# The up-projection of a decoder layer in seeded PSUM banks, with the convolution kept in PSUM

## The chip, the cores and the metric

The kernel runs on one core of one Trainium2 chip. The metric is the device time of one execution in microseconds (us). The profile names the engines PE (TensorE), DVE (VectorE), ACT (ScalarE), POOL (GpSimd) and SP (SyncE, which here issues most transfers). PSUM, the memory into which TensorE writes, is used in eight banks of 128 partitions by 512 floats; SBUF is the memory that the other operands lie in.

## What is computed

One layer of a decoder trunk on 1024 positions of width 1024 in float32: two attention branches, gated and added to the input, then the part that matters here, a gated feed-forward block with a causal depthwise convolution of width 3:

```python
def conv_ffn(xn, w_up, conv_w, conv_b, w_down):
    S = xn.shape[1]
    u = xn @ w_up
    upad = jnp.pad(u, ((0, 0), (CONV_WIDTH - 1, 0), (0, 0)))
    c = conv_b
    for j in range(CONV_WIDTH):
        c = c + upad[:, j:j + S] * conv_w[j]
    gate, val = jnp.split(c, 2, axis=-1)
    return (jax.nn.silu(gate) * val) @ w_down
```

`xn` is the residual stream after an RMS norm, `w_up` is 1024 by 5632 (2816 columns for the gate, 2816 for the value), `w_down` 2816 by 1024. A last RMS norm follows.

## The kernel before

Everything is kept transposed: channels on the 128 partitions, the 1024 positions along the free axis. Each float32 factor is split into a high part of reduced precision (a copy by ScalarE) and a low part (the difference, by VectorE), and a product takes three matmuls per 128 rows of depth: high by high, high by low, low by high (`product`, L828). A matmul has 512 columns.

`hidden` (L839) is the up-projection. It loops over 22 pairs `j`; a pair is one block of 128 gate channels and the matching block of 128 value channels. A pair's two by two blocks (gate and value rows, first and second half of the positions) are computed by Winograd's form of Strassen's scheme, with 7 products of half depth instead of 8. Each product is 12 matmuls into one PSUM bank. In `prods` they are P1 = A11 B11, P2 = A12 B21, P5 = S1 T1, P7 = S3 T3, P3 = S4 B22, P6 = S2 T2 and P4 = A22 T4, where A are blocks of the weights, B of the activations, S sums of A and T sums of B. From pair 1 on TensorE does them in the order P1 P2 P5 P6 P7 P3 P4, the last pair ending with P4 P3.

`recombine` (L389) joins the seven banks: ScalarE copies P1 to SBUF (L395), and seven VectorE operations of 512 columns (L396 to L402) form the four blocks c11, c12 (gate, both halves) and c21, c22 (value). These land in two tiles `us` of 1024 columns, two more at the left for the convolution's past.

`glu` (L950) and `conv` (L962) then work on 1024 columns at a time. For each of the two row blocks GpSimd (VectorE for pair 0's gate) multiplies by the row scale of the norm, `rstd` (L965); ScalarE makes `c` = weight times `us` plus bias (L970); VectorE adds the two other taps (L971, L972). ScalarE applies Silu to the gate's `c` (L957), VectorE multiplies the two (L958), and a transfer on SyncE's queue stores the result to `hd` in DRAM (L959). The row scale itself is spread over the partitions during pair 0, by transposes on TensorE (L173) into two banks.

The weights come from `next_w` (L62) through `ahead`, `sum_pair` (L86) and `split_pair` (L102): two loads per pair (L91 and L93, on SyncE's queue), the four sums S by GpSimd (L96 to L99), casts by ScalarE (L110) and low parts by VectorE (L112). A11 and A12 share one tile `wh` with its low part `wl`; A22 has another; there are two buffers of these, and three for the sums `sh` and `sl`.

The order on each engine is not written out. The framework's scheduler puts the instructions into each engine's queue by priority (program order, raised by `high_priority`) and by when it expects them to be ready; `issue_after` and `add_manual_dep` add edges. On the chip each queue runs in its order and waits by semaphores. The pool `psF` gives TensorE's eight banks under one tag.

`down` (L975) follows: its first stage multiplies blocks of `hd` that are ready by weight pieces (L1023), while the last deferred `glu` calls of the up-projection run.

## Time and profile before

| | us |
|---|---|
| median of 3 runs | 1357.51 (1356.43 to 1357.77) |
| the profiled execution | 1356.2 |
| its span, first to last instruction | 1354.3 |
| pair 1's first matmul, from the span's start | 706.26 |
| the down-projection's first matmul | 1111.07 |

A row of a timeline gives start and duration in us, engine, line, operation, output and inputs, and in brackets the idle time before it with what ended that. A row of a group gives line, engine, operation, shapes and count, then the busy time in us, the mean duration in ns, and the idle time of the engine before them. A row of the waits gives who waited for whom, the total in us, how often, and the longest. A row of the windows gives a stretch, then its length and the busy time (with instructions) of PE, PEld (weight loads), DVE, ACT and POOL, the granted TensorE clock and two figures of the transfers. Where a row names `t`, it is a PSUM bank of the up-projection; B and T name the activation operands, wh, wl, sh, sl the weights.

### The profile page before, as it was taken

The page shows a single profiled execution, that of the slowest core. Times are in us where ns is not written, and L with a number is a line of the kernel's source. Part 1 is how long each engine was busy: PE and PEld are TensorE (multiplying, and loading weights), DVE is VectorE, ACT ScalarE, POOL GpSimd, SP SyncE. Part 2 cuts the span into 40 slices and gives each one's busy share as a digit, 9 for nine tenths or more (in the row PEclk, how much of TensorE's full clock was granted, in tenths as well). Part 3 has the DMA queues.
Part 4 walks back from the last instruction along what each step waited for, and adds up shares of the span by engine and source line. Part 5 has one row for each costly group of instructions (what it writes and reads, how often), then busy time and mean ns, then how long its engine had stood idle before and what let it go on. Part 6 is the DMA issues. An engine that isn't in the chain of part 4 may idle for free.

```text
span 1354.3 us, 17160 instructions
## 1 busy us (share of the span) xinstructions
PE 1335.0 (99%) x6304; PEld 1103.6 (81%) x6304; DVE 1009.8 (75%) x1454; ACT 603.9 (45%) x942; POOL 483.1 (36%) x350
## 2 busy tenths in 40 slices
PE   7999999999999999999999999999999999999997
PEld 6888888888887777878888888888888888888886
DVE  8846775388898875355689888888888898986454
ACT  8422232376667664334444334433443345433343
POOL 0436651010102125741455565555555611231011
PEclk9999999999999999999999999999999999999999
DMA  6334443966554235334422222122212248651342
GB/s 255 140 113 164 143 156 114 272 174 175 156 133 144 77 116 219 117 119 136 166 82 88 71 91 94 62 79 93 93 63 83 92 141 311 215 177 64 94 134 85
DMA packets 62470, 179.50 MB, mean 133 GB/s; under 512 B 6833, under 2 KB 15153, under 8 KB 62385
## 3 DMA queue, kind: packets, MB, share of 16 engines
q1 hardware_dynamic: 50928, 160.98, 36.7%
q10 hardware_dynamic: 11456, 17.41, 3.5%
q8 instruction: 50, 0.82, 0.2%
q14 instruction: 36, 0.29, 0.1%
HBM read 129.61 MB, written 48.76 MB: 132 GB/s over the span
## 4 chain that ended last, share of the span: by engine, by line
PE 62%; DVE 17%; POOL 7%; issue 7%; DMA 4%; ACT 3%; POOLq 0%; DVEq 0%; SPq 0%; ACTq 0%
PE t L836 7%; PE t L837 7%; PE t L835 7%; POOL us L965 3%; PE y L996 3%; PE d L996 3%; PE sc L568 3%; PE g L150 2%; PE g L151 2%; DVE c L958 2%; PE g L152 2%; DVE wl L112 2%; DMA gr<-gd 2%; PE sc L151 2%; PE sc L152 2%
## 5 line engine op out<-in xcount | busy, mean ns | idle before, releaser
L970 ACT ACTIVATE c<-us,vecs 128x1024 f32<-128x1024 f32 x44 | 54.8, 1248 | 163.2 <-POOL us L965 160.0
L965 POOL TENSOR_TENSOR us<-us,rstd 128x1024 f32<-128x1024 f32 x42 | 100.7, 2414 | 52.8 <-DVE wl L131 34.3
L110 ACT CAST sh<-sf 128x1024 fp32r<-128x1024 f32 x62 | 64.9, 1051 | 106.2 <-POOL sf L97 61.8
L129 ACT CAST wh<-raw 128x1024 fp32r<-128x1024 f32 (+2 forms) x60 | 60.7, 1012 | 104.8 <-PE sc L151 33.1
L971 DVE SCALAR_TENSOR_TENSOR c<-us,vecs,c 128x1024 f32<-128x1024 f32 x44 | 67.1, 1527 | 51.9 <-ACT c L970 51.9
L131 DVE TENSOR_TENSOR wl<-raw,wh 128x1024 fp32r<-128x1024 f32 (+2 forms) x60 | 75.3, 1256 | 39.1 <-ACT wh L129 29.3
L96 POOL TENSOR_TENSOR sf<-rv 128x512 f32<-128x512 f32 x30 | 42.5, 1417 | 166.7 <-DMA rv<-in_w_up 73.2
L112 DVE TENSOR_TENSOR sl<-sf,sh 128x1024 fp32r<-128x1024 f32 x62 | 88.3, 1426 | 8.2 <-ACT sh L110 8.2
L167 POOL TENSOR_TENSOR rs<-ms,mhalf 128x8 f32<-128x8 f32 (+2 forms) x9 | 14.5, 1614 | 159.1 <-DVE ms L165 148.5
L150 PE MATMUL g<-xh,wh 128*128 128x512 f32 x176 | 70.7, 402 | 0.1
L152 PE MATMUL g<-xh,wl 128*128 128x512 f32 x176 | 70.4, 400 | 0.0
L151 PE MATMUL g<-xl,wh 128*128 128x512 f32 x176 | 70.4, 400 | 0.0
L98 POOL TENSOR_TENSOR sf<-raw,rv 128x512 f32<-128x512 f32 x30 | 41.6, 1386 | 59.9 <-DVE sl L112 59.9
L572 DVE CUSTOM_DVE_ANT_0 L<-sc,bias 128x128 f32<-128x128 f32 (+7 forms) x64 | 47.7, 752 | 17.4 <-PE sc L568 14.1
L551 POOL MEMSET aT<- 128x128 f32 x32 | 6.1, 204 | 152.0 <-PE t L597 101.6
L573 ACT ACTIVATE L<-L,sm 128x128 f32<-128x128 f32 (+7 forms) x64 | 49.6, 778 | 20.7 <-DVE sm L572 18.2
L97 POOL TENSOR_TENSOR sf<-sf,raw 128x512 f32<-128x512 f32 x31 | 58.0, 1870 | 1.6
L972 DVE SCALAR_TENSOR_TENSOR c<-us,vecs,c 128x1024 f32<-128x1024 f32 x44 | 56.2, 1279 | 0.6
L725 POOL TENSOR_TENSOR gr<-gr,rstd 128x1024 f32<-128x1024 f32 x16 | 39.4, 2467 | 41.4 <-DMA gr<-gd 41.2
L112 DVE TENSOR_TENSOR wl<-raw,wh 128x1024 fp32r<-128x1024 f32 (+1 forms) x35 | 52.8, 1508 | 0.1
L151 PE MATMUL sc<-ml,wh 128*128 128x512 f32 x128 | 50.1, 391 | 0.6 <-DVE ml L746 0.6
L568 PE MATMUL sc<-u,u 128*128 128x512 f32 (+2 forms) x192 | 49.8, 359 | 0.1
(444 smaller groups left out, 4351.4 us busy)
## 6 DMA issues: line engine op xcount, KB each, us to landing
u<-qd SPq DMA_DIRECT2D x72, 256.0 KB, 6.1
raw<-in_w_down SPq DMA_DIRECT2D x27, 512.0 KB, 3.7
raw<-in_w_in SPq DMA_DIRECT2D x25, 512.0 KB, 4.4
hr<-hd SPq DMA_DIRECT2D x50, 256.0 KB, 5.3
raw<-in_w_up SPq DMA_DIRECT2D x23, 512.0 KB, 3.6
hd<-c SPq DMA_DIRECT2D x22, 512.0 KB, 2.8
rv<-in_w_up SPq DMA_DIRECT2D x21, 512.0 KB, 3.5
gr<-gd SPq DMA_DIRECT2D x16, 512.0 KB, 3.6
```

Source lines behind the costliest of these rows:

```text
L112: nc.vector.tensor_tensor(lo, src, hi.bitcast(F32), ALU.subtract)
L131: self.lo = (eng or nc.vector).tensor_tensor(wl, raw, wh.bitcast(F32), ALU.subtract)
L150: nc.tensor.matmul(ps, wh[:, kc + o, :], ah, start=first and n == 0, stop=False)
L151: nc.tensor.matmul(ps, wh[:, kc + o, :], al, start=False, stop=False)
L152: nc.tensor.matmul(ps, wl[:, kc + o, :], ah, start=False, stop=last and n == len(kcs) - 1)
L568: nc.tensor.matmul(sc[:, lo + n0:lo + n1], qs, k[c][part][:, n0:n1], start=part == 0, stop=part == 1)
L835: nc.tensor.matmul(ps, ah[:, k, :], bh, start=first and n == 0, stop=False, skip_group_check=skip)
L836: nc.tensor.matmul(ps, ah[:, k, :], bl, start=False, stop=False, skip_group_check=skip)
L837: nc.tensor.matmul(ps, al[:, k, :], bh, start=False, stop=last and n == len(ks) - 1, skip_group_check=skip)
L965: i = (nc.vector if m % NF == 0 else nc.gpsimd).tensor_tensor(us[:, 2:], us[:, 2:], self.rstd, ALU.mult)
L971: nc.vector.scalar_tensor_tensor(c, us[:, 1:T + 1], cw[1], c, ALU.mult, ALU.add)
L996: nc.tensor.matmul(ps, v[:, n, :], x, start=n == i == 0, stop=n == len(js) - 1 and i == 2)
```

## The change

From pair 1 on the seven products are no longer kept in seven banks and joined by VectorE, but joined as they are made, in four banks a, b, c, d. `begin` makes P1 in a; ScalarE copies a to b (the seed); TensorE makes P5 in d. `chain` adds P6 to b, which then holds P1 + P6; ScalarE copies b to c. TensorE then adds P4 of the pair before to that pair's c, and P2 to a, P7 to c, P3 to b. So its order is P1 P5 P6, P4 of the pair before, P2 P7 P3. VectorE takes the four blocks out of the banks: two are multiplied by the row scale on the way (`scaled`), two get P5 added from a copy `s5` that ScalarE made of d (`summed`) and are then multiplied by the row scale on GpSimd. T4 changes its sign, so that P4 is added; the three lines outside `hidden` do that.

The convolution of pairs 1 to 20 goes in two halves of 512 columns, with `c` in two PSUM banks (`psC`) and not in SBUF; Silu and the gate product read them there. The Silu and the second half's first step are to be issued after the seed of the next pair. The gate block's convolution is called after the next pair's first two products, the value block's after P4. Pair 0 is joined as before. The deferred calls (the value block of pair 20 and both blocks of pair 21) keep their places; those in `down` use SBUF and are no longer scaled there. The pool has seven banks under one tag and one under another, which the sum of squares, the spread of the row scale (both halves in turn) and one bank of `psC` use.

```diff
@@ -284,7 +284,7 @@
                 tt(a, a2, a, ALU.subtract)
                 tt(a2, b2, a2, ALU.subtract)
                 tt(b2, b2, a, ALU.subtract)
-                tt(b, b2, b, ALU.subtract)
+                tt(b, b, b2, ALU.subtract)
 
             def parts(k):
                 for n, r in enumerate((k, k + 4)):
@@ -399,7 +399,7 @@
         tt(c22, ps["P5"], u3, ALU.add)
         tt(u4, ps["P5"], u2, ALU.add)
         tt(c12, ps["P3"], u4, ALU.add)
-        tt(c21, u3, ps["P4"], ALU.subtract)
+        tt(c21, ps["P4"], u3, ALU.add)
 
     def keep(self, m, u, to):
 
@@ -823,7 +823,7 @@
         tt(b12, b22, b12, ALU.subtract)
         put("T13", xw[k])
         tt(t2, b22, b11, ALU.subtract)
-        tt(t4, t2, b21, ALU.subtract)
+        tt(t4, b21, t2, ALU.subtract)
 
     def product(self, ps, a, b, ks=range(4), first=True, last=True, skip=False):
 
@@ -840,15 +840,15 @@
         nc, tc = self.nc, self.tc
         with ExitStack() as ctx:
             e = ctx.enter_context
-            psF = e(tc.tile_pool(name="psF", bufs=8, space=PSUM, reuse_waits="tile"))
-            self.psT = psF
+            psF = self.psT = e(tc.tile_pool(name="psF", bufs=7, space=PSUM, reuse_waits="tile"))
+            self.psC = None
             xc2 = e(tc.tile_pool(name="xc2", bufs=1, side="right", reuse_waits="tile"))
             self.uw = e(tc.tile_pool(name="uw", bufs=3, side="right", reuse_waits="tile"))
             prods = (("P1", "A11", "B11"), ("P2", "A12", "B21"), ("P5", "S1", "T1"), ("P7", "S3", "T3"),
                      ("P3", "S4", "B22"), ("P6", "S2", "T2"), ("P4", "A22", "T4"))
             with tc.high_priority(400):
                 w0 = self.split_pair(*pair)
-            ready = {}
+            ready, prev = {}, None
             for j in range(NF):
                 w, ps = ready.pop(j) if j else (w0, {})
                 if j == 0:
@@ -861,7 +861,7 @@
                         self.B["T4", k], self.B["T2", k] = ((hi[:, c], lo[:, c]) for c in (slice(0, H2), slice(H2, T)))
                     self.tctx.close()
                     tp = e(tc.tile_pool(name="tp", bufs=2, side="right", reuse_waits="tile"))
-                    ssq = self.tl(psF, [P, H2], "t")
+                    ssq = self.tl(psF, [P, H2], "s", bufs=1)
                     for n, (name, a, b) in enumerate(prods[:5]):
                         self.product(ps[name], w[a], b, (3,), first=False)
                         if n == 4:
@@ -876,20 +876,24 @@
                                 h = self.tl(self.uw, [P, 2, H2], ("sh", "sl", "rv", "rv", "sh", "sl")[2 * k + hf], F32R, **({"bufs": 2} if k == 1 else {}))
                                 self.hs[hf, k] = self.split(h[:, 0], h[:, 1], r[:, hf * H2:(hf + 1) * H2])
                         lo = self.lo
-                for name, a, b in (prods[i] for i in ((0, 1, 2, 5, 3, 6, 4) if j == NF - 1 else (0, 1, 2, 5, 3, 4, 6) if j else range(7))):
-                    if name not in ps:
-                        ps[name] = self.tl(psF, [P, H2], "t")
-                        self.product(ps[name], w[a], b)
-                us = [self.tl(tp, [P, T + 2], "us", bufs=3) for _ in range(2)]
-                if j == NF - 1:
-                    self.defer.pop(0)(lo)
-                    self.xctx2.close()
-                    self.uw = None
-                    self.open_down()
-                    self.deep = True
-                    with tc.high_priority(100):
-                        self.ahead(2)
-                self.recombine(ps, us, tp, 2)
+                if j == 0:
+                    for name, a, b in prods:
+                        if name not in ps:
+                            ps[name] = self.tl(psF, [P, H2], "t")
+                            self.product(ps[name], w[a], b)
+                    us = [self.tl(tp, [P, T + 2], "us", bufs=3) for _ in range(2)]
+                    self.recombine(ps, us, tp, 2)
+                else:
+                    us, last = self.chain(w, ps or self.begin(psF, w), tp, prev)
+                    if j == NF - 1:
+                        self.defer.pop(0)(lo)
+                        self.xctx2.close()
+                        self.uw = None
+                        self.open_down()
+                        self.deep = True
+                        with tc.high_priority(100):
+                            self.ahead(2)
+                        last()
                 if j < NF - 1:
 
                     w, ps = ready[j + 1] = self.next_w(), {}
@@ -897,21 +901,76 @@
                         raw = [self.tl(self.sfp[0], [P, T], "t42", bufs=1)] + [self.tl(self.sfp[0], [P, T], "sf") for _ in range(2)]
                         for k, r in enumerate(raw):
                             nc.sync.dma_start(r, self.hd[k])
-                    for name, a, b in prods[:2 if j == 0 else 0]:
-                        ps[name] = self.tl(psF, [P, H2], "t")
-                        self.product(ps[name], w[a], b)
                 if j == 0:
+                    ps.update(self.begin(psF, w))
                     for hf in range(2):
-                        sp = self.tl(psF, [P, H2], "t")
+                        sp = self.tl(psF, [P, H2], "s", bufs=1)
                         self.spread(sp, rs, hf * 4)
                         nc.scalar.copy(self.rstd[:, hf * H2:(hf + 1) * H2], sp)
 
-                for w in range(2):
-                    f = lambda after=None, j=j, w=w, us=us: self.glu(j, w, us[w], tp, after)
-                    if j + w < NF - 1:
-                        f()
-                    else:
-                        self.defer.append(f)
+                first, second = (lambda after=None, j=j, w=w, us=us: self.glu(j, w, us[w], after, j > 0) for w in range(2))
+                if j == NF - 1:
+                    self.defer += [first, second]
+                elif j == 0:
+                    first()
+                    second()
+                else:
+                    prev = first, last, second
+                    if j == NF - 2:
+                        self.defer.append(second)
+                        prev = first, last, lambda: None
+            self.psC = None
+
+    def begin(self, pool, w):
+
+        ps = {n: self.tl(pool, [P, H2], "t") for n in "adbc"}
+        self.product(ps["a"], w["A11"], "B11", skip=True)
+        self.seed = self.nc.scalar.copy(ps["b"], ps["a"])
+        self.product(ps["d"], w["S1"], "T1")
+        return ps
+
+    def chain(self, w, ps, tp, prev):
+
+        nc = self.nc
+        tt = nc.vector.tensor_tensor
+        a, b, c, d = (ps[n] for n in "abcd")
+        us = [None, None]
+
+        def half(r, hf):
+            if us[r] is None:
+                us[r] = self.tl(tp, [P, T + 2], "us", bufs=3)
+            return us[r][:, 2 + hf * H2:2 + hf * H2 + H2], self.rstd[:, hf * H2:(hf + 1) * H2]
+
+        def scaled(r, hf, p):
+            u, rs = half(r, hf)
+            tt(u, p, rs, ALU.mult)
+
+        def summed(r, hf, p):
+            u, rs = half(r, hf)
+            tt(u, p, s5, ALU.add)
+            nc.gpsimd.tensor_tensor(u, u, rs, ALU.mult)
+
+        s5 = self.tl(tp, [P, H2], "s1", bufs=1)
+        nc.scalar.copy(s5, d)
+        if prev:
+            self.psC = [self.tl(self.psT, [P, H2], "s", bufs=1), self.tl(self.psT, [P, H2], "t")]
+            prev[0]()
+        self.product(b, w["S2"], "T2", first=False, skip=True)
+        nc.scalar.copy(c, b)
+        for f in prev[1:] if prev else ():
+            f()
+        self.product(a, w["A12"], "B21", first=False, skip=True)
+        scaled(0, 0, a)
+        self.product(c, w["S3"], "T3", first=False, skip=True)
+        summed(1, 1, c)
+        self.product(b, w["S4"], "B22", first=False, skip=True)
+        summed(0, 1, b)
+
+        def last():
+            self.product(c, w["A22"], "T4", first=False, skip=True)
+            scaled(1, 0, c)
+
+        return us, last
 
     def open_down(self):
         tc = self.tc
@@ -947,30 +1006,41 @@
         tt(b21, b22, b21, ALU.subtract)
         self.B["T4", k] = self.parts_h(b21)
 
-    def glu(self, j, w, us, tp, after):
-
-        nc = self.nc
-        c = self.conv(j + w * NF, us, tp, after)
+    def glu(self, j, w, us, after, scaled):
+
+        nc = self.nc
         if w == 0:
-            self.c0 = c
+            self.c0 = self.tl(self.cpl, [P, T], "c")
+        for c, a, b in self.conv(j + w * NF, us, after, scaled):
+            g = self.c0[:, a:b]
+            if w == 0:
+                with self.tc.issue_after(self.seed.ins) if self.psC else nullcontext():
+                    nc.scalar.activation(g, c, AF.Silu)
+            else:
+                nc.vector.tensor_tensor(g, g, c, ALU.mult)
+        if w == 0:
             return
-        nc.scalar.activation(self.c0, self.c0, AF.Silu)
-        nc.vector.tensor_tensor(self.c0, self.c0, c, ALU.mult)
         store = lambda c0=self.c0: nc.sync.dma_start(self.hd[j], c0)
         self.late.append(store) if after is not None else store()
 
-    def conv(self, m, us, tp, after=None):
+    def conv(self, m, us, after, scaled):
         nc = self.nc
         nc.gpsimd.memset(us[:, 0:2], 0.0)
-        i = (nc.vector if m % NF == 0 else nc.gpsimd).tensor_tensor(us[:, 2:], us[:, 2:], self.rstd, ALU.mult)
-        if after is not None:
-            self.tc.add_manual_dep(i.ins, after.ins.name, mybir.DependencyInfo(mybir.DependencyClass.Sync, mybir.DependencyReason.DATA), reason="later")
-        c = self.tl(self.cpl, [P, T], "c")
+        if not scaled:
+            (nc.vector if m % NF == 0 else nc.gpsimd).tensor_tensor(us[:, 2:], us[:, 2:], self.rstd, ALU.mult)
         cw = [self.vecs[:, C_CW + 3 * m + k:C_CW + 3 * m + k + 1] for k in range(3)]
-        nc.scalar.activation(c, us[:, 2:], AF.Identity, bias=self.vecs[:, C_CB + m:C_CB + m + 1], scale=cw[2])
-        nc.vector.scalar_tensor_tensor(c, us[:, 1:T + 1], cw[1], c, ALU.mult, ALU.add)
-        nc.vector.scalar_tensor_tensor(c, us[:, 0:T], cw[0], c, ALU.mult, ALU.add)
-        return c
+        for a, b in ((0, H2), (H2, T)) if self.psC else ((0, T),):
+            if self.psC:
+                c = self.psC[a // H2]
+            else:
+                c = self.c0 if m < NF else self.tl(self.cpl, [P, T], "c")
+            with self.tc.issue_after(self.seed.ins) if self.psC and a else nullcontext():
+                i = nc.scalar.activation(c, us[:, 2 + a:2 + b], AF.Identity, bias=self.vecs[:, C_CB + m:C_CB + m + 1], scale=cw[2])
+            if after is not None:
+                self.tc.add_manual_dep(i.ins, after.ins.name, mybir.DependencyInfo(mybir.DependencyClass.Sync, mybir.DependencyReason.DATA), reason="later")
+            nc.vector.scalar_tensor_tensor(c, us[:, 1 + a:1 + b], cw[1], c, ALU.mult, ALU.add)
+            nc.vector.scalar_tensor_tensor(c, us[:, a:b], cw[0], c, ALU.mult, ALU.add)
+            yield c, a, b
 
     def down(self):
 
@@ -982,6 +1052,7 @@
             self.uw = e(tc.tile_pool(name="uwd", bufs=2, side="right", reuse_waits="tile"))
             self.hpb = e(tc.tile_pool(name="hpb", bufs=HPB, side="right", reuse_waits="tile"))
             self.sfp = self.cpl, "c"
+            self.psC = None
             self.B = {}
             tt = nc.vector.tensor_tensor
             bank = lambda n: self.tl(psD, [P, H2], "dy"[n])
```

## The prediction, made before the changed kernel had run

> **What bounds the kernel now.** I read the page first, then the busy time by windows, then TensorE's rows around the pairs of the up-projection, then the waits and the chain in that stage.
>
> ```profile
> span 1354.3 us, 17160 instructions
> PE 1335.0 (99%) x6304; PEld 1103.6 (81%) x6304; DVE 1009.8 (75%) x1454; ACT 603.9 (45%) x942; POOL 483.1 (36%) x350
> ```
>
> The profiled execution took 1356.2 us, 1.9 us more than its span; the median of the three runs is 1357.5, 1.3 above it. TensorE is busy for 99% of the span, so whatever the change does to VectorE, ScalarE and GpSimd counts only through the time in which TensorE stands still. The question is how much of that lies where the change works: from the start of pair 1 (the second) to the first matmul of the down-projection.
>
> ```profile
> 706.26 0.39 PE L835 MATMUL t<-B_0h,wh 128*128 128x512 f32 x1
> 1111.07 0.62 PE L1023 MATMUL d<-sh,wh 128*128 128x512 f32 x2
> 711.70 0.49 PE L173 MATMUL t<-ident,rs 128*128 128x128 f32 x3
> 712.49 0.48 PE L835 MATMUL t<-T_0h,sh 128*128 128x512 f32 x1
> 1254.05 5.44 PE d L996 x24
> ```
>
> The first two rows enclose 404.8 us. The last, from the chain, says what TensorE needs when nothing stops it: 24 matmuls of 512 columns in 5.44 us, 0.2267 each. A pair has 7 products of 12 matmuls, 84, or 19.04 us; 21 pairs take 399.8. The transposes that spread the row scale take 712.49 - 711.70 = 0.8. So 404.8 - 399.8 - 0.8 = 4.2 us are lost in the whole stretch. **That is all that there is to win here**, 0.31% of the time.
>
> ```profile
> 918.09 0.39 PE L835 MATMUL t<-B_0h,wh 128*128 128x512 f32 x1
> 937.44 0.39 PE L835 MATMUL t<-B_0h,wh 128*128 128x512 f32 x1
> 938.02 0.18 PEld L837 LDWEIGHTS t<-B_0h,wl 128*128 128x128 f32 x1 [0.39 <-DVE wl L112]
> ```
> ```profile
> PEld t L837 <- DVE wl L112: 5.7, 14, 0.5
> DVE c L971 <- ACT c L970: 49.7, 22, 2.8
> ACT sh L110 <- POOL sf L97: 56.3, 18, 4.9
> ```
>
> One pair lasts 937.44 - 918.09 = 19.35, which is 0.31 over its matmuls. The third row is the place: the third matmul of the pair waits for the low part of its weights, written by VectorE. By the waits between 706 and 1111 us this happens 14 times; 14 x 0.3 is the 4.2 again. Why is VectorE late with weights whose buffer came free 14 us earlier? The chain shows it:
>
> ```profile
> 925.38 2.92 POOL us L965
> 928.33 1.26 ACT c L970
> 929.64 1.61 issue
> 931.86 1.27 DVE c L972
> 936.25 1.72 DVE wl L112
> 937.96 2.23 DVE c L958
> 944.73 2.92 POOL us L965
> ```
>
> It repeats every 944.73 - 925.38 = 19.35 us and has no matmul in it: GpSimd scales a row block, ScalarE starts the convolution, VectorE works through convolution, weights, gate and recombination, and only then can GpSimd scale the next. This ring, not TensorE's 19.04, sets the pace from the eighth pair on, where the first of the 14 waits stands.
>
> **The change part by part.** The busy times of pair 1's stretch and of a window of 8 later pairs (us, then TensorE, weight loads, VectorE, ScalarE, GpSimd), and the groups of that window:
>
> ```profile
> 706.00:725.50 19.50, 19.50 (x91) 16.22 (x90) 19.21 (x19) 10.66 (x12) 11.74 (x9) 1.00 0.27 82
> 918.10:1072.80 154.70, 154.64 (x674) 125.75 (x673) 132.70 (x129) 59.83 (x64) 87.56 (x65) 1.00 0.25 81
> L971 DVE SCALAR_TENSOR_TENSOR c<-us,vecs,c 128x1024 f32<-128x1024 f32 x16 | 24.0, 1499 | 20.6 <-ACT c L970 20.6
> L972 DVE SCALAR_TENSOR_TENSOR c<-us,vecs,c 128x1024 f32<-128x1024 f32 x16 | 20.5, 1280 | 0.3
> L958 DVE TENSOR_TENSOR c<-c,c 128x1024 f32<-128x1024 f32 x8 | 18.4, 2306 | 0.0
> L112 DVE TENSOR_TENSOR wl<-raw,wh 128x1024 fp32r<-128x1024 f32 x9 | 16.0, 1780 | 0.0
> L396 DVE TENSOR_TENSOR us<-t,s 128x512 f32<-128x512 f32 x8 | 5.5, 685 | 0.0
> L970 ACT ACTIVATE c<-us,vecs 128x1024 f32<-128x1024 f32 x16 | 20.0, 1249 | 61.4 <-POOL us L965 61.4
> L110 ACT CAST sh<-sf 128x1024 fp32r<-128x1024 f32 x16 | 16.8, 1051 | 23.9 <-POOL sf L97 23.9
> L957 ACT ACTIVATE c<-c 128x1024 f32<-128x1024 f32 x8 | 8.5, 1063 | 9.3 <-DVE c L972 9.3
> L110 ACT CAST wh<-raw 128x1024 fp32r<-128x1024 f32 x8 | 8.3, 1034 | 0.0
> L395 ACT COPY s<-t 128x512 f32<-128x512 f32 x8 | 4.5, 565 | 0.0
> L965 POOL TENSOR_TENSOR us<-us,rstd 128x1024 f32<-128x1024 f32 x16 | 38.9, 2452 | 1.1
> L96 POOL TENSOR_TENSOR sf<-rv 128x512 f32<-128x512 f32 x8 | 10.4, 1300 | 42.5 <-DMA rv<-in_w_up 37.1 <-DVE c L972 5.4
> ```
>
> And from the whole span, what the new half-width forms come nearest to:
>
> ```profile
> L627 DVE SCALAR_TENSOR_TENSOR y<-y,subw,t 128x512 f32<-128x512 f32 x8 | 5.9, 743 | 1.2 <-PE t L173 1.2
> L1089 ACT ACTIVATE x<-x,vecs 128x512 f32<-128x512 f32 x14 | 10.1, 724 | 0.4
> L796 ACT ACTIVATE t<-x 128x512 f32<-128x512 f32 x14 | 8.4, 618 | 0.0
> ```
>
> *TensorE*: the same 84 matmuls, regrouped; nothing added. The sign of T4 only exchanges operands: nothing. *VectorE*: 7 recombining operations of 0.685 become 4, which saves 2.1. The convolution's four of 1.50 and 1.28 (5.6) become eight halves: no row has one that reads and writes PSUM; 0.64 (half of 1.28) and 0.74 (L627) are the two ends, 5.1 to 5.9; I take 0.74, the row with a PSUM operand. The gate product, 2.31, becomes two of 0.68 with one operand in PSUM, 1.4. VectorE's 132.7 / 8 = 16.6 falls by 2.1 + 0.9 and grows by 0.4: to 14.0, against 19.04 of TensorE. *GpSimd*: two of 2.45 become two of about 1.30 (L96): 10.9 to 8.6. *ScalarE*: one copy of 0.57 becomes three; two biased copies of 1.25 become four of 0.72; one Silu of 1.06 two of 0.62: 7.5 to 9.2. Nothing here reaches 19. The ring is opened: half of each row block is scaled by VectorE straight out of PSUM, so ScalarE no longer waits there for GpSimd, and a pair's last product is joined inside the next pair.
>
> So TensorE should run at its own pace: **minus 4.2**, if none of the new waits is late. These are worked out with 2.72 us per product (12 x 0.2267), counted from the pair's start; order P1, P5, P6, P4 of the pair before, P2, P7, P3.
>
> - The seed, ScalarE's copy of P1's bank, may be done while P5 runs: 2.72, of which it needs 0.57: slack 2.1 us. A late seed holds P6 and every matmul queued behind it, and on ScalarE the second half of the convolution and the Silu, which are made to follow it, with VectorE's steps behind those.
> - The second seed (P6's bank) has P4 and P2 before P7 needs it: slack 5.44 - 0.57 = 4.9.
> - P4 of the pair before adds to a bank that VectorE read after P7 of that pair; three products lie between. Cost nothing.
> - The weights of P1 and P2 share a buffer that comes free after P2. P2 moves from second to fifth place, so the window to the next pair shrinks from 5 products to 2, 5.44 us, plus 0.45 until the first low part is used. Cast 1.03 and low part 1.78 need 2.8: slack 3.1, which one or two operations of VectorE ahead of it (0.7 each) leave positive.
> - Convolution in PSUM takes a bank of its own and one of the seven; with four per pair and one left of the pair before, six of the seven are held. Cost nothing.
> - The spread of the row scale has one bank for its two halves; the second waits for ScalarE's copy, 0.5 us, unless P6 goes ahead of it. Bounds 0 and 0.6; I take 0.3, once.
> - The second pair's weights fall into the time in which VectorE still does pair 0 the old way (19.2 of 19.5 us busy in the first windows' row). Bounds 0 and 2; I take 0.4, once.
> - SyncE's queue keeps its transfers. A weight load waits for the low part of the weights whose buffer it fills, so it moves with P2 or P4 by up to three products (8.2 us), and what it brings is used a pair later, 19 us. The down-projection's first weights get their buffer three products before use. Cost nothing.
>
> Sum: -4.2 + 0.3 + 0.4 = -3.5; 1356.2 - 3.5 = 1352.7 for the profiled execution, 1354.0 by the median. Should the cover of the seed go, each us that it is late costs 20 us, for there are 20 pairs after it.
>
> **The rivals.**
>
> *Slower: the seed stands behind a waiting cast.* ScalarE's rows show that it does its instructions in the order in which they were queued, waiting ones included:
>
> ```profile
> 921.11 0.39 PE L835 MATMUL t<-B_0h,wh 128*128 128x512 f32 x1
> 931.44 0.56 ACT L395 COPY s<-t 128x512 f32<-128x512 f32 x1
> ```
>
> This copy needs only P1, and the first row is the start of P2, the product after it; the copy came 10 us later, because other work stood ahead. Today nobody waits for that copy; after the change TensorE does. What could stand ahead is the cast of the weight sums, which idles 23.9 / 8 = 3.0 us per pair for GpSimd's L97. If that wait begins as P1 ends, the seed is done 3.0 + 1.05 + 0.57 = 4.6 us later, 1.9 beyond P5: 20 x 1.9 = 38 us, 1392 in all. If it begins 1.5 us earlier, 0.4 per pair: +8, less the 3.5, 1362. It decides from the point where more than 2.1 us lie between P1's end and the seed's start. [...] Against it: GpSimd has 2.3 us less to do, and the convolution's later parts are made to follow the seed.
>
> *No gain: the weights stay late.* If VectorE has the second row block's convolution (six operations, 4.2 us) ahead of the low part, cast and wait make 1.0 + 4.2 + 1.8 = 7.0 against 5.9, so 1 us per pair is lost, +17; with four of them ahead the wait is 0 to 0.3 as today: 1357.5.
>
> *It doesn't do what it says*: an order that puts the products or the convolution back where they were leaves the ring, and 1357.5.
>
> **How the numbers follow.** The case that TensorE's pace holds gets 0.55. It is worth 3.5 us, 4.2 at most, and the mark of 0.2% (2.7 us, about what a measurement of this kernel can tell from no change) is near: 0.45 of it is faster, 0.10 the same. Seed late: 0.25, slower. Weights late: 0.15, of which 0.05 is slower. No effect: 0.05. So faster 0.45, same 0.25, slower 0.30. The low end is 1357.5 - 4.2 and 0.8 for the spread of the runs, 1352.5. The high end leaves out the worse half of the slower cases, 0.15: 1357.5 - 3.5 + 20 x 0.7 = 1368. The likeliest case alone is 1353 to 1355.5.
>
> **What would show it.** Right: the wait of TensorE's weight load for "wl L112" gone, pairs 19.04 to 19.1 apart, VectorE near 14 us per pair, GpSimd near 8.6, the chain in this stage made of matmuls. Wrong: TensorE waiting for a scalar copy at the head of P6 (the seed), or still for wl with a longer wait; pairs above 19.4 apart; half-width convolution steps above 0.9 us. My forecast fails if any wait comes back in every pair with 0.2 us or more.

## The result and the profile after

The changed kernel takes 1367.47 us (median of 6 runs, 1366.98 to 1369.09) against 1357.1 before (6 runs): a ratio of 1.0079, 95% interval 1.0066 to 1.0092. It is **slower by about 10 us**. That lies in the forecast range, near its upper end, but on the other side of the forecast; the range reached so far up only through the rivals, so that the time falls inside it says nothing for the mechanism forecast. The profiled execution took 1367.48 us. First a line of its page, then rows of TensorE around the pairs:

```profile
PE 1338.8 (98%) x6304; PEld 1101.8 (81%) x6304; DVE 947.0 (69%) x1491; ACT 638.3 (47%) x1044; POOL 429.0 (31%) x350
```
```profile
705.93 0.39 PE L835 MATMUL t<-B_0h,wh 128*128 128x512 f32 x1
710.02 0.32 PE L173 MATMUL s<-ident,rs 128*128 128x128 f32 x1 [1.18 <-POOL rs L167]
720.97 0.50 PE L835 MATMUL t<-B_0h,wh 128*128 128x512 f32 x1 [1.45 <-ACT wh L110]
730.52 0.50 PE L835 MATMUL t<-T_0h,wh 128*128 128x512 f32 x1 [1.02 <-DVE us L950]
785.05 0.39 PE L835 MATMUL t<-B_0h,wh 128*128 128x512 f32 x1
1100.29 0.39 PE L835 MATMUL t<-B_0h,wh 128*128 128x512 f32 x1
1122.61 0.62 PE L1094 MATMUL d<-sh,wh 128*128 128x512 f32 x2
```

VectorE has 63 us less to do (1009.8 before) and GpSimd 54 (483.1), both a little more than forecast, and the time rose all the same. From pair 1's start to the down-projection's first matmul are now 1122.61 - 705.93 = 416.7 us, 11.9 more than the 404.8 of before, so the whole loss lies in the changed stretch. Over the floor of 399.8 + 0.8 it loses 16.0. The marks split this: up to the start of pair 5 (785.05) stand 27 products (four pairs less the P4 still owed), 73.4 us, and the spread; 79.12 - 73.4 - 0.8 = **4.9 at the start**, nearly all in the three waits shown, after which pairs 3 and 4 run at 19.04. The next 16 pairs take 315.24 us, 19.70 each, **10.6 over the floor**; the last adds 0.6. Most of the 16 last 19.5 to 19.7 us, two last 20.22.

What stops TensorE in those pairs, by the waits from 705 to 1125 us, with four waits of the other engines and of SyncE's queue (SPq) ahead (who waited for whom, total, times, longest):

```profile
SPq L93 <- DVE wl L112: 257.8, 19, 15.3
POOL sf L96 <- DMA rv<-in_w_up: 198.2, 18, 12.4
ACT t L1038 <- POOL us L951: 57.1, 20, 2.9
ACT sh L110 <- POOL sf L97: 28.0, 19, 4.9
PE t L835 <- ACT t L959: 3.4, 14, 0.3
PE t L835 <- ACT t L928: 0.5, 2, 0.3
```

L959 is the second seed, the copy of P6's bank that P7 adds to; L928, the first seed, held TensorE twice. The wait for `wl L112` is gone, but for a single one of 0.2 by a weight load. The forecast had given the second seed 4.9 us of slack. Rows of one pair:

```profile
911.60 0.39 PE L837 MATMUL t<-T_3h,sl 128*128 128x512 f32 x1
915.80 1.04 ACT L110 CAST sh<-sf 128x1024 fp32r<-128x1024 f32 x1
916.74 0.59 ACT L959 COPY t<-t 128x512 f32<-128x512 f32 x1
917.38 0.50 PE L835 MATMUL t<-T_0h,sh 128*128 128x512 f32 x1 [0.18 <-ACT t L959]
```

The first row is P6's last matmul; P6 ends at 912.0. P4 (eleven of its twelve matmuls; the scheduler put the first ahead of P5) and P2 keep TensorE busy until 917.04, where P7 was due; but the copy runs only at 916.74, because ScalarE's queue had a Silu, a copy, a bias of the convolution and the cast of weight sums ahead of it, and these were late. TensorE restarts at 917.38, 0.34 us late, and its next row comes 0.34 instead of 0.23 us later: some 0.45 us in all, of which the profile calls 0.18 idle. Why they were late stands in the chain, the view that follows work back to what released it. Here is one turn of it, in order of time, from 890 to 960 us, with the shorter steps left out where three points stand:

```profile
899.78 3.49 DMA rv<-in_w_up
903.43 1.29 POOL sf L96
...
907.31 1.29 POOL sf L99
908.68 3.02 POOL us L951 x2
911.72 0.79 ACT t L1038
...
913.33 0.77 DVE t L1042
914.12 0.60 ACT c L1018
...
915.88 0.97 ACT sh L110
...
918.02 0.68 DVE us L946
918.70 0.61 DVE wl L112
919.33 3.51 DMA rv<-in_w_up
```

This is a **new ring**, 919.33 - 899.78 = 19.55 us, with no matmul in it. The load of the second half of a pair's weights takes 3.65 to GpSimd's start; the four weight sums 5.25; the two row scalings, behind them in GpSimd's queue, 3.04; a bias, the two taps, a Silu and the copy `s5` behind it, 3.36; the next bias and the cast of the sums 1.83; on VectorE the low part of those sums, a row scaling and at last the low part of A22's weights 2.42. That last step frees the buffer `rv`, for which the next load has been waiting (the first row of the waits): there are two such buffers, and the chain closes. The two pairs of 20.22 us fit it: the transfers in their turns, at 780.95 and 1017.46, took 4.63 and 4.19 us where the others around them took 3.5.

### The profile page after: what moved, and what is told of

Its sections match the earlier page's. It is cut to its first block, busy times and chain, and to the rows that moved or that the text cites. A ratio compares the mean times of both kernels' runs of the same rounds, so it can differ in the third digit from the quotient of the medians.

```text
span 1365.7 us, 17239 instructions
## 1 busy us (share of the span) xinstructions
PE 1338.8 (98%) x6304; PEld 1101.8 (81%) x6304; DVE 947.0 (69%) x1491; ACT 638.3 (47%) x1044; POOL 429.0 (31%) x350
## 4 chain that ended last, share of the span: by engine, by line
PE 60%; POOL 13%; DVE 11%; DMA 7%; ACT 5%; issue 4%; POOLq 0%; SPq 0%; ACTq 0%; DVEq 0%
PE t L835 6%; PE t L836 6%; PE t L837 6%; DMA rv<-in_w_up 4%; POOL us L951 3%; PE y L1067 3%; PE d L1067 3%; PE sc L568 3%; PE g L150 2%; PE g L151 2%; PE g L152 2%; DMA gr<-gd 2%; PE sc L151 2%; PE sc L152 2%; PE sc L150 2%
## 5 line engine op out<-in xcount | busy, mean ns | idle before, releaser
L112 DVE TENSOR_TENSOR sl<-sf,sh 128x1024 fp32r<-128x1024 f32 x62 | 91.7, 1482 | 84.8 <-ACT sh L110 73.6
L1038 ACT ACTIVATE s<-us,vecs 128x512 f32<-128x512 f32 x40 | 31.3, 783 | 98.0 <-DVE us L946 98.0
L951 POOL TENSOR_TENSOR us<-us,rstd 128x512 f32<-128x512 f32 x42 | 63.8, 1537 | 16.1 <-DVE us L950 16.1
L1038 ACT ACTIVATE t<-us,vecs 128x512 f32<-128x512 f32 x40 | 31.6, 790 | 57.5 <-POOL us L951 57.1
L1041 DVE SCALAR_TENSOR_TENSOR t<-us,vecs,t 128x512 f32<-128x512 f32 x40 | 30.1, 752 | 39.7 <-ACT t L1038 39.7
L152 PE MATMUL sc<-mh,wl 128*128 128x512 f32 x128 | 49.8, 389 | 0.0
L150 PE MATMUL sc<-mh,wh 128*128 128x512 f32 x128 | 49.8, 389 | 0.0
L99 POOL TENSOR_TENSOR sf<-raw,sf 128x512 f32<-128x512 f32 x31 | 44.9, 1448 | 1.6
```

The source lines that it names most:

```text
L112: nc.vector.tensor_tensor(lo, src, hi.bitcast(F32), ALU.subtract)
L150: nc.tensor.matmul(ps, wh[:, kc + o, :], ah, start=first and n == 0, stop=False)
L152: nc.tensor.matmul(ps, wl[:, kc + o, :], ah, start=False, stop=last and n == len(kcs) - 1)
L951: nc.gpsimd.tensor_tensor(u, u, rs, ALU.mult)
```

## The experiments

All are edits of the changed kernel but one. Theory A: the ring above, closed by the second weight load and its buffer, sets the pace; it exists because P4, deferred from the end of its pair to the fourth place of the next, holds the weights of A22 four products (10.9 us) longer. The two rivals that the runs were chosen against: ScalarE's amount of work or order by itself (C), and the convolution in PSUM (D). Each run is compared, by the ratio, with the kernel before as measured beside it (1354.75 to 1355.53 us). The load, the sums and the row scalings are read at lines that move by a few from kernel to kernel.

**A third buffer `rv`**, once in the changed kernel, once in the kernel before. The space comes from three places: the mix's squares get one buffer for three, `u4` takes `s1`'s place, and one held column moves to another pool. (`rv` holds the loaded second half of a pair's weights; two texts on record call it a buffer for the low parts.)

```diff
-v = ... self.tl(self.uw, [P, 2, 4, P], idle or "rv", bufs=2)
+v = ... self.tl(self.uw, [P, 2, 4, P], idle or "rv", bufs=3)
```

> The changed kernel with the same third buffer for rv. Theory A: pairs go from 19.6 to 19.04-19.15 us from the sixth pair on, about 9 us less; the losses in the first two pairs (about 5 us) stay: 1357.5-1360 us. Rival C (ScalarE's added copies and halved steps are simply too much work in order, whatever the load does): the second seed stays late, 1366-1368 us.

1355.04 (11 runs) against 1355.53 before: ratio 0.9997 (0.9988 to 1.0006), 11 us below what the changed kernel takes by its ratio (1.0079 of 1355.53, 1366.2), and a little better than the range expected. No matmul waits for the second seed, and the windows of 818.69 to 975.71 us, eight pairs of the changed kernel, differ so; the changed kernel first, then this one (length, then PE, PEld, DVE, ACT, POOL, clock, transfers):

```profile
818.69:975.71 157.02, 155.22 (x673) 125.28 (x672) 106.95 (x144) 72.92 (x105) 65.50 (x64) 1.00 0.24 81
```
```profile
818.69:975.71 157.02, 157.02 (x694) 130.02 (x693) 116.41 (x152) 76.94 (x106) 65.12 (x66) 1.00 0.26 87
```

TensorE is busy without a gap, and ScalarE's queue from pair 1 on has the very order that it has in the changed kernel, instruction by instruction, as the two timelines show; the order by itself is thus not the cause. On GpSimd two of the four sums changed places. The stretch takes 1109.90 - 706.10 = 403.8: what is lost is at the start.

As a control, the same space with two buffers:

> The changed kernel with the space rearranged as in the run with three buffers for the low parts (squares of the mix in one buffer, u4 in s1's place, 18 and 10 held columns), but with two buffers, as it had. If the third buffer is what gave 12 us there, this one stays with the changed kernel: 1366 to 1369, pairs of 19.5 to 19.65 with TensorE waiting for the second seed. If the rearranged space gave them, it comes near 1355.

1365.98 (ratio 1.0087, 1.0071 to 1.0102), with the wait for the second seed back 12 times: the rearranged space gives nothing, the third buffer does.

> The kernel before, with a third buffer for the second weight load (rv) during the up-projection; its space comes from other pools (the squares' buffers in the mixing stage 3 to 1, one recombination buffer shared, the h parts 18 + 10 instead of 19 + 9). Theory A (a ring through the second weight load paces both kernels: low part of A22, load of rv, four sums on GpSimd, row scale on GpSimd, convolution on ScalarE and VectorE, low part of A22): the load starts a pair earlier, the ring is cut, pairs go from 19.35 to 19.04-19.1 us, the wait for wl goes, 1353-1354.5 us. Rival B (VectorE's amount of work is the ring, as the prediction had it): pairs stay at 19.35, 1356.5-1358 us.

The kernel before with the buffer: 1370.17 (1.0111, 1.0097 to 1.0125), slower, which neither theory had expected. Its chain:

```profile
932.85 1.84 POOL us L967
934.72 1.25 ACT c L972
...
953.00 1.82 POOL us L967
```

One turn is 953.00 - 932.85 = 20.15, and no load is in it (the chain passes through one in the next turn, at 960.95, and that turn is no longer): it is the ring of the prediction, GpSimd's scaling, ScalarE, VectorE and back. It is longer because the scheduler, with the buffer free earlier, put two sums between the two row scalings on GpSimd. That the ring of the kernel before needs no load is read from its own chain, in the prediction; this run is no test of that, since the order changed with the buffer.

**One GpSimd sum done twice per pair**, the order of all engines otherwise unchanged:

```diff
 tt(sa[:, 0], v[:, 0], v[:, 1], ALU.add)
+if self.twice:
+    tt(sa[:, 0], v[:, 0], v[:, 1], ALU.add)
```

> The changed kernel with the first of the four weight sums on GpSimd done twice in each pair of the up-projection (same result, one more operation of 1.27 us per pair). Theory A: it stands in the ring, so pairs go from 19.6 to 20.8-20.9 us as soon as the ring paces, over 15 to 17 pairs: 1386-1391 us. Rival C: GpSimd idles over 10 us in each pair, so 1367-1369 us.

1392.49 (1.0272 of before): 26 us above the changed kernel by the ratios and a little above the expected range, for one operation of 1.3 us per pair, though GpSimd is busy for only 68.2 of the 157.0 us of the window above. The turn of the ring, read at the first sum:

```profile
915.86 1.29 POOL sf L96
...
936.66 1.33 POOL sf L96
```

936.66 - 915.86 = 20.80, 1.25 more than 19.55: the whole of the added sum, nothing of it hidden. The turns beside it are longer, 21.50 (with a slower transfer, 3.91) and 20.97. TensorE now waits at the first seed too, 17 times, up to 1.6 us.

**P4 back in its own pair**, as the last of its seven, all else in the program as changed:

```diff
+        if own:
+            last()
+            return us, lambda: None
         return us, last
```

> The changed kernel with P4 back in its own pair: P1 P5 P6 P2 P7 P3 P4, all else as changed. P4 then ends about 10.9 us earlier than behind the next pair's P6, and with it the buffer of its low part comes free, the second weight load starts, and GpSimd's sums follow. Theory A (the ring through that load): the wait for the second seed goes, pairs 19.04 to 19.1 unless P4 itself has to wait, 1355 to 1358. P4 adds to a bank that VectorE reads after P7, one product (2.72) before: if VectorE is over 2 us late there, a new wait of 0.2 to 1 us per pair stands at P4 and the time is 1359 to 1376. If the deferral has nothing to do with it, 1366 to 1368.

1359.31 (1.0033, 1.0020 to 1.0046), 6.7 us below what the changed kernel takes by the ratios (1.0079 of 1355.29, 1366.0). That is above the 1355 to 1358 expected without a wait at P4. The per-pair wait is gone, the window of eight pairs is full, and the cast of A22's weights comes at the start of the pair instead of 13.8 us into it (917.26 - 903.43 in the changed kernel, whose pair began at 903.43):

```profile
818.69:975.71 157.02, 157.02 (x694) 130.05 (x693) 119.87 (x150) 77.51 (x107) 70.09 (x66) 1.00 0.25 84
```
```profile
729.17 0.50 PE L835 MATMUL t<-T_0h,wh 128*128 128x512 f32 x1 [3.33 <-DVE us L950]
923.58 0.63 ACT L110 CAST wh<-rv 128x512 fp32r<-128x512 f32 x1 [1.61 <-PE t L836]
923.61 0.39 PE L835 MATMUL t<-B_0h,wh 128*128 128x512 f32 x1
938.40 1.10 POOL L951 TENSOR_TENSOR us<-us,rstd 128x512 f32<-128x512 f32 x1
```

The first row is what keeps it behind the others: the second pair's P4 stood 3.3 us for VectorE, which was still at pair 0. With the start mended as below it takes 1354.59 (0.9996). One reservation: with P4 moved, the scheduler also put the work of the other three engines in another order, on GpSimd the row scalings one at a time and not together. In the changed kernel itself the cast comes 2.9 us after P4's end, behind the second seed in ScalarE's queue. So the run shows that the ring goes when P4 comes back, not how much of that is the buffer held longer and how much the order.

**The row scaling on VectorE alone.** GpSimd scales the second half of each row block (the texts on record call it the first); here VectorE does that too:

```diff
 tt(u, p, s5, ALU.add)
-nc.gpsimd.tensor_tensor(u, u, rs, ALU.mult)
+tt(u, u, rs, ALU.mult)
```

> The changed kernel with the first half of each row block scaled by VectorE (about 0.7 us) instead of GpSimd (1.5 us): GpSimd has 3.0 us less per pair, and nobody on the ring waits for GpSimd to get to the scaling behind the four sums; VectorE has 1.4 us more, some 14.8 of 19.04. Theory A (ring through the second weight load and GpSimd's queue): the sums no longer stand ahead of the convolution, the ring falls by 1.5 us or more, below 19.04, pairs 19.04 to 19.1, 1356 to 1360. Rival C (ScalarE's order, in which the second seed stands behind casts that wait for the sums, without any part of the row scaling): the sums come when they came, pairs 19.5, 1366 to 1368.

1355.10 (1.0003, 0.9994 to 1.0012). No matmul waits in the later pairs. The load and the sums are still late (the first sum comes 16.0 us after its pair's start, in the changed kernel only as the next pair starts), but nothing queues behind them:

```profile
L951 DVE TENSOR_TENSOR us<-us,rstd 128x512 f32<-128x512 f32 x17 | 19.8, 1163 | 0.3
931.92 1.29 POOL L96 TENSOR_TENSOR sf<-rv 128x512 f32<-128x512 f32 x1 [13.25 <-DMA rv<-in_w_up]
926.74 0.62 ACT L110 CAST wh<-rv 128x512 fp32r<-128x512 f32 x1 [0.65 <-PE t L836]
```

VectorE pays more for the two scalings than expected, 1.16 us each and not 0.7, and has the room. GpSimd idles 13.25 us for the transfer, and the cast waits for P4 in the next pair (0.65 us for PE), at 926.74, 10.85 us after that pair's start at 915.89. That is four products, the deferral.

**The second seed on VectorE**:

```diff
-nc.scalar.copy(c, b)
+nc.vector.tensor_copy(c, b)
```

> The changed kernel with the second seed copied by VectorE instead of ScalarE. Theory A: the copy no longer stands behind ScalarE's cast of the sums; if VectorE does it soon after P6, TensorE waits at P7 no more and the pairs come to 19.04 to 19.15, 1357 to 1360; but where VectorE's own order puts it behind the convolution, which waits for the same sums by way of the row scaling, the wait at P7 stays, pairs 19.3 to 19.6, 1362 to 1369. Rival C (ScalarE's order alone) says 1356 to 1358 in either case.

1371.21 (1.0124, 1.0110 to 1.0138), slower still, and above every range expected. 8.4 us are lost at one place that neither theory named: the second pair's copy stands behind VectorE's work for pair 0. In the later pairs the chain is:

```profile
904.60 3.51 DMA rv<-in_w_up
908.27 1.28 POOL sf L96
...
924.16 3.43 DMA rv<-in_w_up
```

924.16 - 904.60 = 19.56, the same ring to a hundredth, without the second seed. The wait only shows elsewhere: TensorE's weight loads now stop for `wl` (12 times, 5.8 us in all, from 760 to 1120 us) and for VectorE's sums with P5 (L950: 13 times, 3.7 us). Rival C, as it stood (1356 to 1358), falls: the copy was where the ring met TensorE, not part of it. ScalarE's bias, Silu and cast are part of it.

**The convolution back in SBUF**, 1024 columns at a time, the seeded banks kept:

```diff
-self.psC = [self.tl(self.psT, [P, H2], "s", bufs=1), self.tl(self.psT, [P, H2], "t")]
```

> The changed kernel with the convolution back in SBUF at 1024 columns, the products still joined in seeded banks. Theory A: the ring holds a full-width ScalarE step and full-width VectorE steps where it had halves, so pairs of 19.6 us or up to 1 us more: 1367-1385 us. Rival D (it is the convolution in PSUM, in halves and behind the seed, that costs): pairs near 19.1 us, 1357-1361 us.

1450.99 (1.0703), far above what both expected. Its chain turns in 24.1 us (873.30 - 849.23), with a pause and the sums (two of them much longer, 2.33 and 2.23) ahead of the row scalings:

```profile
849.23 3.06 POOL us L951 x2
...
856.41 9.62 issue
...
873.30 3.05 POOL us L951 x2
```
```profile
866.07 2.33 POOL L96 TENSOR_TENSOR sf<-rv 128x512 f32<-128x512 f32 x1 [9.66 <-DMA rv<-in_w_up]
```

The 9.62 us of "issue" are the load again: GpSimd's own row, the last shown, names the transfer into `rv`, which SyncE issued at 862.3, behind the low part of A22's weights at 861.6. So this is theory A's ring with longer steps (a bias of 1.25, taps of 1.30, a Silu of 1.06) and with a wait of ScalarE for TensorE in it (0.55 at 858.30); the first seed holds TensorE 14 times between 760 and 1120 us, 44.5 us in all. TensorE's granted clock is 0.92 in the window of 818.69 to 975.71 us, where it is 1.00 in the changed kernel. D falls, since the loss grows without the PSUM convolution; what the width, the place and the order are worth apart is not shown, because the edit also drops the edges that put Silu and the second half behind the seed.

**The start.** Three edits: the spread of the row scale behind P5 of the second pair, the first half of pair 0's gate behind that pair's second seed, its second half behind the pair's P3.

```diff
+with tc.issue_after(self.mm.ins):
     self.spread(sp, rs, hf * 4)
...
-first()
-second()
+self.pre = [first, second]
...
+with self.tc.issue_after(self.seed2.ins):
+    self.pre.pop(0)()
...
 summed(0, 1, b)
+if self.pre:
+    self.pre.pop(0)()
```

A first form, on the kernel with three buffers, had both halves behind the second seed:

> The changed kernel with three buffers for the low parts (which ran at 1355.0), with two edits at the start of the seeded pairs: the row scale is spread only after P5 of the second pair, and the first pair's gate is issued behind the second seed of the second pair. There TensorE lost 1.0 + 0.6 at the spreads and 1.45 at the second pair's weights. If those are waits for GpSimd's row scale and for ScalarE's order, as the rows say, 2 to 3 us go: 1352 to 1353.5. If they only move to the next instruction, 1354.5 to 1355.5.

1354.05 (0.9994, 0.9985 to 1.0003), 0.4 us gained by the ratios and none in the stretch (1108.35 - 704.56 = 403.8): the weights' wait went, the second spread waited 1.05 for ScalarE and P4 1.06 for VectorE instead. With the second half later, first on P4 in its own pair, then on the kernel with the scaling on VectorE:

> The same, with three edits at the start of the seeded pairs: the row scale spread behind P5 of the second pair, the first pair's first half of the gate issued behind that pair's second seed, its second half behind that pair's P3. They aim at the waits of 1.2 (spread), 1.6 (the second pair's weights) and 1.2 us (P4 behind VectorE) in the runs before. All three gone: 3 to 4 us below the same kernel without them. If they only move, as one of them did in the last run of this kind (1.6 and 1.2 taken out or moved gave 1.0), 0 to 1.5 us.

> The changed kernel with the first row scaling on VectorE (1355.1 beside 1354.75 of the kernel before) and the same three edits at the start. Its 4.0 us of waits are all at the start, one each of 1.2, 1.6 and 1.2: if all go, 1351; if the second spread still waits for ScalarE, 1352.3; if they only move, 1354 to 1355.

The first of these takes 1354.59 (0.9996, 0.9987 to 1.0005), 4.7 us less than without the edits, though P4 still waits 1.52 us for VectorE. The last takes 1352.30 (8 runs) against 1355.29: **0.9977, 0.9967 to 0.9987, below both kernels**. Its stretch:

```profile
704.35 0.39 PE L835 MATMUL t<-B_0h,wh 128*128 128x512 f32 x1
1106.42 0.61 PE L1099 MATMUL d<-sh,wh 128*128 128x512 f32 x2
```

1106.42 - 704.35 = 402.07, 1.4 over the floor of 400.6. The time is the one expected for a second spread that still waits, but that is mostly luck: of the spread only a weight load waits, 0.3 us, and the one matmul wait of the stretch is 0.45 us for `wl`, at 723.18.

## Why the prediction was wrong

*What there was to win* was right: 4.2 us over the floor, of which the best version gets 2.7 in this stretch (404.8 - 402.07). The ring named for the kernel before is in that kernel's chain; no run tests it.

*The work per engine* was right. Per pair in the window of eight VectorE has 13.4 (14.0 forecast), ScalarE 9.1 (9.2), GpSimd 8.2 (8.6). The half steps of the convolution in PSUM, for which there was no row, and the halves by GpSimd and ScalarE:

```profile
L951 POOL TENSOR_TENSOR us<-us,rstd 128x512 f32<-128x512 f32 x16 | 24.4, 1546 | 0.0
L1038 ACT ACTIVATE t<-us,vecs 128x512 f32<-128x512 f32 x16 | 12.6, 790 | 23.4 <-POOL us L951 23.4
L1042 DVE SCALAR_TENSOR_TENSOR t<-us,vecs,t 128x512 f32<-128x512 f32 x16 | 12.0, 753 | 0.3
L96 POOL TENSOR_TENSOR sf<-rv 128x512 f32<-128x512 f32 x8 | 10.4, 1298 | 91.0 <-DMA rv<-in_w_up 79.5 <-DVE wl L112 11.4
```

VectorE's half step takes 0.75 against 0.74 forecast; ScalarE's bias 0.79 against 0.72; GpSimd's scaling 1.55 against 1.30.

*"The ring is opened"* was half right. The old one is: ScalarE and VectorE start on half of a row block without GpSimd. The other half still goes through GpSimd's queue.

*"SyncE's queue keeps its transfers ... Cost nothing"* is **the step that failed**. It asked when the load's product is used by TensorE, a pair later, and found 19 us of room. It did not ask what is queued behind the first instruction that waits for the load. That is GpSimd's first sum, and the prediction had quoted its row: 37.1 us of idle time for this very transfer in eight pairs, 4.6 per pair, already before the change; now it is 79.5, 9.9 per pair. It also put the shift of P4 at three products at most, 8.2 us; it is four, 10.9. Behind that sum stand three more and then the row scalings, which ScalarE and VectorE need in this pair. The runs that cut this path at three different places (a third buffer, P4 in its own pair, the scaling off GpSimd) each brought the eight pairs to TensorE's pace, and the one that lengthened it by 1.25 us paid that in full. With the prediction's own prices (four sums 5.2, two halves 2.6, two biases 1.44, two taps 1.48, Silu 0.62, cast 1.05) and 3.65 and 2.42 from the chain for the transfer and VectorE's last steps, the ring comes to 18.5 against TensorE's 19.04: next to no room. That the two halves on GpSimd took 0.2 longer each, that ScalarE's copy `s5` stands behind the Silu (0.36) and that the other steps came out some 0.3 longer together made it 19.55.

*"The second seed ... slack 4.9"* failed with it: the sum counted the products between P6 and P7, not what ScalarE's queue holds ahead of the copy. The copy was done at 917.33, 5.3 us after P6's end, where 5.0 were left.

*The first seed*, the weights of P1 and P2, the banks: right. TensorE waited twice for the seed, 0.3 each, in the two pairs of 20.22 us, and once 0.2 for `wl`. The two runs with longer rings, the doubled sum and the convolution in SBUF, did stop at the seed, up to 1.6 and 3.4 us by the waits between 760 and 1120 us.

*The start* was mis-sized: 0.7 for the spread and the second pair's weights; the three waits of 1.2, 1.45 and 1.0, with TensorE's restarts, made 4.9. The bounds given, 0.6 and 2, did hold the second of them, not the spread (it waited for GpSimd's row scale itself, not for a bank) and not P4 behind VectorE.

*The rival that was slower* came nearest: it had a seed stuck in ScalarE's queue behind work that waits for GpSimd. But the cast that waits for the sums (28.0 us above) stands ahead of the first seed, which stopped TensorE only twice. The seed that stopped it in 14 pairs is the second, and ScalarE was late there by its wait for the row scaling, 57.1 us in 20 times. Why GpSimd was late, the load, the rival did not have. The rows of 915.80 and 916.74 show ScalarE working in the order of its queue: a copy ready since 912.0 runs at 916.74, back to back behind the cast.

## What to carry to other kernels

When a step is moved later, follow the buffer that it holds: who fills it next, which instruction waits first for that, and what is queued behind that instruction on its engine. Add up such a path once round, with the transfer in it; if it comes within a few per cent of the pace of the bounding engine (here 18.5 by the prices against 19.04), it may well set the pace (here 19.55), whatever the busy shares say. An engine that takes work out of a queue with a waiting instruction at its head can be worth more than less work: two scalings of 1.16 us added to VectorE in each pair took the 3.04 us of the two on GpSimd out of the ring.

## What was not expected of the hardware

A pair became longer by the full 1.25 us of the doubled GpSimd sum although GpSimd was busy for 43% of the window: here GpSimd's queue bounds the kernel by what waits in it, not by its share. And GpSimd's row scaling of 512 columns took 1.55 us in the changed kernel and 1.10 in the one with P4 in its own pair (the last row shown of it). Two rows of the changed kernel and one of the kernel with three buffers:

```profile
908.35 1.33 DVE L112 TENSOR_TENSOR sl<-sf,sh 128x1024 fp32r<-128x1024 f32 x1 [1.17 <-ACT sh L110]
908.64 3.05 POOL L951 TENSOR_TENSOR us<-us,rstd 128x512 f32<-128x512 f32 x2
916.57 2.27 POOL L953 TENSOR_TENSOR us<-us,rstd 128x512 f32<-128x512 f32 x2 [3.38 <-DVE us L952]
```

The neighbour on the same engine is not it: with three buffers two run back to back and take 2.27 together. What differs is who starts first. In the changed kernel VectorE's low part of the sums starts 0.3 us ahead, takes 1.33, and the two scalings need 3.05; with three buffers the scalings start first, and the low part, at 918.25, takes 1.68 (1.22 where GpSimd stands idle). The scaling moved to VectorE behaves alike: 1.78 us at 915.66, just behind the start of a sum on GpSimd at 915.61, and 0.68 at 919.61 with GpSimd idle. In all these rows the one that starts second is the longer; no run varied that alone.
